# Seven RMS norms of an encoder trunk: the mean of squares and its root over the full tile width instead of one-column sums

## The chip, the core and the metric

The kernel runs on one core of one Trainium2 chip, in one launch. The metric is device time in microseconds (us) from the start of the program to its end; smaller is better. The names of the engines are those of the profile: PE is the matrix engine (TensorE), DVE the vector engine, ACT the scalar engine, POOL is GpSimd, SP issues most of the DMAs. Each engine works through its own queue in order.

## The reference

One encoder layer is applied to two groups of tokens, a prompt of 1024 and a sample of 256, each with 256 memory tokens of its own, at a width of 1024 features, all in fp32.

```python
def rmsnorm(x, w):
    y = x * lax.rsqrt(jnp.mean(x * x, -1, keepdims=True) + EPS)      # EPS = 1e-6
    return y * w

def encoder_layer(x, mem, ...):
    h = rmsnorm(x, norm_mix_w)
    ...                                  # gated DeltaNet and gMLP branches, both of h
    x = x + merged @ w_out
    x = x + memory_cross_attention(rmsnorm(x, norm_xa_w), rmsnorm(mem, norm_mem_w), ...)
    h = rmsnorm(x, norm_ffn_w)
    gu = h @ ffn_w_gate_up
    return x + (silu(gu[..., :D_FF]) * gu[..., D_FF:]) @ ffn_w_down

y = rmsnorm(trunk(x), final_norm_w)      # for prompt and sample
```

The gMLP branch holds a layer norm over 512 features (`layernorm(gelu(v))`), which the change does not touch, but whose instructions stand close to one of the seven norms.

## The kernel before

**Layout.** Features lie on the 128 partitions, in 8 tiles (`k` or `m` from 0 to 7), and tokens along the free axis. The 1280 tokens are cut into three blocks: block 0 and block 1 are 512 prompt tokens each, block 2 is the 256 sample tokens. A norm therefore adds over partitions, and that sum is made on PE.

**Products.** PE multiplies either in fp32 or in the format float32r. Large products are three float32r products: `split` (L124 to L126) has ACT copy a tile to its rounded part `hi` (or `whi`) and DVE or POOL subtract to get the rest `lo` (`wlo`), and PE adds hi·hi, hi·lo and lo·hi in one PSUM bank. Every product goes through `mm`, so nearly all of PE's rows carry line L108.

**A norm before.** `Norm.add` (L240 to L255) squares one of the 8 tiles on ACT into `nsq` (L253; the first directly into the accumulator `nacc`, L250) and adds it to `nacc` on DVE (L254). `Norm.rest` does the remainder, for 512 tokens: four sums of one column each, `nacc` times a column of ones in fp32 (L268; the profile shows two records for each, `bank<-cst,nacc` 128x1); on DVE the mean and EPS (L271) and `rsqrt` (L225 to L230), an integer guess and three Newton steps in ten instructions on 128x4 numbers, into `nst`; four fp32 products with the identity that spread the four columns over all partitions (L276, `bank<-cst,nst` 128x128); then for each of the 8 tiles one DVE product x·w·rstd (L289), and a `sink` that uses the normalised tile (a split into `hi` and `lo` for the products that follow, or a store). With 256 tokens there are two columns instead of four.

**What sets the order.** PE's order is written out by hand: a `main` generator of the large products, and `side` generators, which `pump` resumes when `K.clock`, an estimate of PE's own time advanced by `mm`, has passed the time that they asked for (`yield lag`, in ns). The norms are such side generators; their `lag` and `lag2` place the sums and the spreading products among the large products. The order on DVE, ACT and POOL is made by the scheduler at build, from its own model, so a changed norm can also reorder instructions that are not its own.

**The seven norms that the change touches**, in order of time: x1, the mix norm of block 1 (`norm`, L306 to L312, called at L462, with a lag of 4500); mem, the memory norm (called at L466), whose input `mem` is loaded into the buffer that x1's input leaves (L356, one buffer) and which starts when x1 is done; the FFN norms of blocks 0, 1 and 2 (L1497, in `OutProj.run`), with `inplace`, where the second wait `LAGS2` is 9500 ns for blocks 1 and 2; and the final norms of block 1 and block 0 (L2267), with `LAGF2` 9000. The other norms stay: x0 (L458), the first sample norm (L403 to L424), the three norms of the cross-attention (`rstd_of`, L293) and the final sample norm (L2269 on). The first and the last sample norm already use a seed from ACT (`Abs_reciprocal_sqrt`) and a Newton step over their whole width.

**Neighbours that matter.** While x1 and mem run, PE works on the input products of the gMLP branch, and DVE on its GELU (L487 and L489, `gt` and `ug`) and its layer norm (`ln`, L505 to L518: sums over `vg`, small operations on `sums` 128x4, again `rsqrt` L226 to L230, and at L518 the four wide operations that write `vg`). PE's products `sw`·`vg` (L627) need these. While the FFN norm of block 1 runs, block 2 is still being projected: each of its 8 tiles is added to the residual on DVE (L1462), squared on ACT and added to `nacc` (L254). At the same time POOL splits FFN weights (`wlo<-raw,whi`, 128x1024, L126) and makes four sums of weights (L1847, `raw<-raw`), which the `after` function (L1835 to L1848) issues, and `make_r1` (L1865 to L1869) makes differences of the normalised blocks (L1867, `x<-x,x`) for the FFN's fast product scheme and splits them. In the final norms, half of the eight tiles (`SHARED`) are scaled on ACT and POOL, the others on DVE.

## Time and profile before

| | |
|---|---|
| Time, median of 3 runs (lowest, highest) | 2190.44 us (2190.17, 2190.68) |
| Time of the profiled execution | 2190.45 us |
| Span of the profiled execution | 2188.7 us |
| Granted clock of the core | 0.999 |
| ACT busy | 879.9 us (40%) |
| POOL busy | 569.7 us (26%) |

The span is the time from the first to the last instruction of the profile, 1.75 us less than the execution's own time; the profiled execution is 0.01 us from the median. All times of rows are counted from the start of the span. A row of a group names the line, the engine, the operation, what is written and read (`out<-in`), the shape, the count, then the busy time and the mean duration of one in ns, and idle time ahead of it. A row of the timeline begins with the start and the duration in us; `x4` means that four instructions in a row are put together, the duration reaching from the first start to the last end. Products on PE overlap: what one costs is not its duration but the distance from its start to the start of the next.

### The profile page before, as it was taken

To read this page: it belongs to the slowest core of one execution; us is meant where nothing else is said; L and a number is where in the kernel's file an instruction comes from. 1 tells how busy PE (TensorE), PEld (TensorE's weight loads), DVE (VectorE), ACT (ScalarE), POOL (GpSimd) and SP (SyncE) were. 2 spreads that over 40 slices of the span, in tenths; PEclk is the share of its full clock that TensorE was granted. 3 is DMA by queue.
4 is the path that set the end of the run, shared out by engine and by line. 5 is a ranking of instruction groups with operands and counts; after the bars stand their busy time and mean duration, and the time that the engine had idled before them with its cause. 6 is when DMAs were issued, how large, how long until landed. Compare 5 with 4: busy or idle time off the path is not lost.

```text
span 2188.7 us, 32379 instructions
## 1 busy us (share of the span) xinstructions
PE 2174.0 (99%) x12436; PEld 1905.0 (87%) x12436; DVE 1354.3 (62%) x2614; ACT 879.9 (40%) x1649; POOL 569.7 (26%) x379
## 2 busy tenths in 40 slices
PE   9999999999999999999999999999999999999998
PEld 8988888898888899888988888888888888888888
DVE  7867587686874855677644556644434444378575
ACT  6533262544535553224544533332322323343454
POOL 2010010100000000142412332566666665200031
PEclk9999999999999999999999999999999999999999
DMA  5221412323234546741512521222222222493631
GB/s 194 92 93 58 119 56 91 81 66 93 75 118 126 168 139 202 243 147 39 192 67 97 171 100 63 102 84 87 82 77 78 84 97 92 143 349 120 206 111 58
DMA packets 188309, 255.13 MB, mean 117 GB/s; under 512 B 71978, under 2 KB 102266, under 8 KB 188154
## 3 DMA queue, kind: packets, MB, share of 16 engines
q1 hardware_dynamic: 170618, 228.15, 31.7%
q10 hardware_dynamic: 17536, 24.91, 3.1%
q8 instruction: 97, 1.59, 0.3%
q14 instruction: 58, 0.48, 0.1%
HBM read 179.05 MB, written 73.97 MB: 116 GB/s over the span
## 4 chain that ended last, share of the span: by engine, by line
PE 92%; DVE 5%; ACT 2%; DMA 1%; issue 1%; SPq 0%; POOL 0%; DVEq 0%; ACTq 0%
PE bank L108 91%; PE bank L121 1%; DVE acc L690 1%; DVE U L932 1%; DMA braw<-gq 1%; DMA raw<-in_w_sv 0%; DVE zt L924 0%; ACT U L914 0%; ACT UT L911 0%; DVE nt L289 0%; DVE gb L811 0%; DVE gs L690 0%; ACT junk L513 0%; ACT acc L688 0%; DVE lo L126 0%
## 5 line engine op out<-in xcount | busy, mean ns | idle before, releaser
L108 PE MATMUL bank<-hi,whi 128*128 128x512 f32 (+1 forms) x1976 | 701.2, 355 | 0.2 <-DVE vg L489 0.2
L108 PE MATMUL bank<-lo,whi 128*128 128x512 f32 (+1 forms) x1976 | 686.8, 348 | 0.0
L108 PE MATMUL bank<-hi,wlo 128*128 128x512 f32 (+1 forms) x1976 | 686.8, 348 | 0.0
L108 PEld LDWEIGHTS bank<-hi,wlo 128*128 128x128 f32 x1976 | 373.6, 189 | 48.2
L108 PEld LDWEIGHTS bank<-hi,whi 128*128 128x128 f32 x1976 | 374.4, 189 | 44.4 <-DVE vg L489 1.0
L108 PEld LDWEIGHTS bank<-lo,whi 128*128 128x128 f32 x1976 | 374.5, 190 | 42.8
L125 ACT ACTIVATE whi<-raw 128x1024 fp32r<-128x1024 f32 (+1 forms) x136 | 136.9, 1009 | 248.6 <-PE bank L108 218.9
L126 POOL TENSOR_TENSOR wlo<-raw,whi 128x1024 fp32r<-128x1024 f32 x65 | 158.4, 2439 | 295.5 <-ACT whi L125 295.5
L108 PE MATMUL bank<-bhl,whi 128*128 128x512 f32 x408 | 125.9, 390 | 0.0
L126 DVE TENSOR_TENSOR wlo<-raw,whi 128x1024 fp32r<-128x1024 f32 (+1 forms) x71 | 80.7, 1139 | 70.5 <-ACT whi L125 70.3
L126 POOL TENSOR_TENSOR wlo<-x,whi 128x1024 fp32r<-128x1024 f32 x40 | 96.5, 2412 | 47.5 <-ACT whi L125 47.5
L2107 DVE TENSOR_TENSOR x<-x,bank 128x512 f32<-128x512 f32 x21 | 14.5, 689 | 125.1 <-ACT x L1902 125.1
L690 DVE SCALAR_TENSOR_TENSOR acc<-craw,sm,acc 128x510 f32<-128x510 f32 (+1 forms) x96 | 73.8, 769 | 27.6 <-ACT acc L688 25.9
L108 PEld LDWEIGHTS bank<-bhl,whi 128*128 128x128 f32 x408 | 76.4, 188 | 16.4 <-ACT whi L125 0.4
L1915 DVE SCALAR_TENSOR_TENSOR t<-t,x 128x512 f32<-128x512 f32 x42 | 63.9, 1520 | 28.4 <-ACT t L1914 28.4
L125 ACT ACTIVATE whi<-x 128x1024 fp32r<-128x1024 f32 (+1 forms) x48 | 49.2, 1025 | 77.2 <-PE bank L108 69.3
L108 PE MATMUL bank<-bhl,wlo 128*128 128x512 f32 x204 | 79.6, 390 | 0.5 <-DVE wlo L126 0.5
L108 PE MATMUL bank<-bhl,ahl 128*128 128x512 f32 x312 | 75.0, 395 | 0.0
L1924 DVE SCALAR_TENSOR_TENSOR t<-bank,t 128x512 f32<-128x512 f32 (+1 forms) x44 | 24.5, 558 | 81.4 <-PE bank L108 81.4
L1051 ACT ACTIVATE gs<-bank 128x512 f32<-128x512 f32 (+1 forms) x60 | 31.2, 519 | 103.2 <-PE bank L108 93.8
L1902 ACT ACTIVATE x<-bank 128x512 f32<-128x512 f32 x63 | 37.7, 599 | 82.8 <-PE bank L108 80.1
L108 PEld LDWEIGHTS bank<-bhl,ahl 128*128 128x128 f32 x312 | 58.7, 188 | 13.7
(416 smaller groups left out, 4513.5 us busy)
## 6 DMA issues: line engine op xcount, KB each, us to landing
raw<-in_w_gu SPq DMA_DIRECT2D x44, 512.0 KB, 3.4
braw<-gq SPq DMA_DIRECT2D x14, 1024.0 KB, 6.4
raw<-in_w_g SPq DMA_DIRECT2D x20, 512.0 KB, 3.3
gq<-t SPq DMA_DIRECT2D x33, 256.0 KB, 2.0
gtd<-gs ACTq DMA_DIRECT2D x32, 256.0 KB, 2.4
w<-in_w_dn SPq DMA_DIRECT2D x8, 1024.0 KB, 11.0
raw<-in_w_qkv SPq DMA_DIRECT2D x12, 512.0 KB, 3.5
gq<-r SPq DMA_DIRECT2D x22, 256.0 KB, 2.0
```

Of the source, the lines that this page charges most:

```text
L108: self.nc.tensor.matmul(out, l, r, start=start, stop=stop, skip_group_check=more)
L121: self.nc.tensor.transpose(out, x, ident)
L125: self.last_hi = self.nc.scalar.activation(hi, src, AF.Copy).ins
L126: (eng or self.nc.vector).tensor_tensor(out=lo, in0=src, in1=f32(hi), op=ALU.subtract)
L690: V.scalar_tensor_tensor(out=dst, in0=src, scalar=wj, in1=dst, op0=ALU.mult, op1=ALU.add)
L932: V.scalar_tensor_tensor(out=U[d][:, hs, :], in0=quad(pu), scalar=mine[:, 2 * level + d : 2 * level + d + 1], in1=U[d][:, hs, :], op0=ALU. ...
L1051: S.activation(t, ps, AF.Tanh, scale=0.5)
L1902: S.activation(t, ps, AF.Copy)
L1915: V.scalar_tensor_tensor(out=t, in0=t, scalar=1.0, in1=src, op0=ALU.add, op1=ALU.mult)
L1924: V.scalar_tensor_tensor(out=out, in0=u, scalar=sign, in1=t, op0=ALU.mult, op1=ALU.mult)
L2107: V.tensor_tensor(out=c22, in0=c22, in1=pe, op=ALU.add)
```

## The change

`rest` gets an argument `wide`, set for the seven norms named above. `wide` splits the accumulator at once into two float32r tiles, `nhi` (ACT) and `nlo` (DVE), in the buffers that held squares; waits `lag` + 1500 ns of PE's clock; and makes two products over the whole width with a tile of 1/1024 in all places (`means`, a column `mean_r` read 128 times), whose sum is the mean of squares on every partition. ACT takes the seed of the root of the mean and EPS from it (`Abs_reciprocal_sqrt`), into the accumulator, and DVE makes one Newton step in three wide instructions. The eight products x·w·rstd and the sinks are as before. The four sums of one column, the ten small DVE instructions, the second wait (`LAGS2`, `LAGF2`) and the spreading products go. The `nst` tile of the first part has one buffer instead of two.

```diff
+        def room(self, name, dt=F32):
+            return self.p.tile([P, 512], dt, tag="nsq", name=name, bufs=self.sq)[:, : self.n]
+
+        def wide(self, xk, wcol, sink, pace, shared, lag, ks, inplace, ready):
+
+            n = self.n
+            parts = [self.acc] if self.apart is None else [self.acc, self.apart]
+            hls = []
+            for x in parts:
+                hi, lo = self.room("nhi", F32R), self.room("nlo", F32R)
+                split(hi, lo, x, V)
+                hls += [hi, lo]
+            yield lag + 1500
+            pb = bank()[:, :n]
+            for t in hls:
+                mm(pb, means, t, t is hls[0], t is hls[-1])
+            while ready is not None and not ready():
+                yield 300
+            r = self.acc
+            S.activation(r, pb, AF.Abs_reciprocal_sqrt, bias=eps)
+            V.scalar_tensor_tensor(out=pb, in0=pb, scalar=EPS, in1=r, op0=ALU.add, op1=ALU.mult)
+            V.scalar_tensor_tensor(out=pb, in0=pb, scalar=-0.5, in1=r, op0=ALU.mult, op1=ALU.mult)
+            V.scalar_tensor_tensor(out=pb, in0=pb, scalar=1.5, in1=r, op0=ALU.add, op1=ALU.mult)
...
@@ norm: x1 and mem
-        yield from nm.rest(xk, wcol, sink, pace, lag=lag)
+        yield from nm.rest(xk, wcol, sink, pace, lag=lag, wide=True)
...
+    mean_r = tail.tile([P, 1], F32R, name="mean_r")
+    means = mean_r.to_broadcast([P, P])
     S.activation(h05[:, 12:13], mean, AF.Abs_reciprocal_sqrt)
+    V.tensor_copy(mean_r, mean)
...
@@ the FFN norms of three blocks
-                    norm_b = nms[b].rest(xk, wcol, sinks(b, hs), PACES[b], ks=range(KT) if b != 1 else SECOND_KS, inplace=True, lag2=LAGS2[b])
+                    norm_b = nms[b].rest(xk, wcol, sinks(b, hs), PACES[b], ks=range(KT) if b != 1 else SECOND_KS, inplace=True, wide=True)
...
@@ the final norms of blocks 1 and 0
-            K.side(nm.rest(lambda k: x2[b][:, k, :], S_FIN, sink, PACEF, SHARED[b], LAGF[b], lag2=LAGF2[b]))
+            K.side(nm.rest(lambda k: x2[b][:, k, :], S_FIN, sink, PACEF, SHARED[b], LAGF[b], wide=True))
```

The lines of the changed kernel are up to 42 numbers higher than the old ones (L518 is now L560, L1462 is L1504, L1867 is L1909, the products of L289 are at L328). The change also moves instructions that are not the norms' own. Two places matter below.

**DVE around the gMLP's layer norm of block 0.** `sums` are the small operations of its root (L228 to L230, three Newton steps), `vg` its result, `gt` and `ug` belong to the GELU, and `nacc<-nacc,nsq` are the additions of the mem norm's squares. DVE's queue before:

```order
L228 SCALAR_TENSOR_TENSOR sums<-sums 128x4
L229 TENSOR_TENSOR sums<-sums 128x4
L487 SCALAR_TENSOR_TENSOR gt<-gt,bank 128x512
L230 SCALAR_TENSOR_TENSOR sums<-sums 128x4
L126 TENSOR_TENSOR lo_121<-nt,hi_120 128x512
L228 SCALAR_TENSOR_TENSOR sums<-sums 128x4
L489 SCALAR_TENSOR_TENSOR ug<-gt,bank 128x512
L229 TENSOR_TENSOR sums<-sums 128x4
L230 SCALAR_TENSOR_TENSOR sums<-sums 128x4
L518 TENSOR_SCALAR vg<-vg,sums 128x512 x4
L487 SCALAR_TENSOR_TENSOR gt<-gt,bank 128x512
L254 TENSOR_TENSOR nacc<-nacc,nsq 128x512 x2
```

And of the change, at the same place:

```order
L254 TENSOR_TENSOR nacc<-nacc,nsq 128x512
L229 TENSOR_TENSOR sums<-sums 128x4
L531 SCALAR_TENSOR_TENSOR ug<-gt,bank 128x512
L230 SCALAR_TENSOR_TENSOR sums<-sums 128x4
L254 TENSOR_TENSOR nacc<-nacc,nsq 128x512
L228 SCALAR_TENSOR_TENSOR sums<-sums 128x4
L254 TENSOR_TENSOR nacc<-nacc,nsq 128x512
L229 TENSOR_TENSOR sums<-sums 128x4
L254 TENSOR_TENSOR nacc<-nacc,nsq 128x512
L230 SCALAR_TENSOR_TENSOR sums<-sums 128x4
L254 TENSOR_TENSOR nacc<-nacc,nsq 128x512
L560 TENSOR_SCALAR vg<-vg,sums 128x512 x4
```

Before, the four `vg` stood ahead of all additions of the mem norm; now five of its seven additions stand ahead of them.

**DVE at the end of block 2's projection.** `x_12569` (before) and `x_12549` (after) are block 1, being normalised; `x_12570` and `x_12550` are block 2, whose additions are the 256 wide ones. The queue before, from the last residual addition of block 2 on:

```order
L1462 SCALAR_TENSOR_TENSOR x_12570<-bank,x_12570 128x256
L126 TENSOR_TENSOR lo_12883<-x_12569,hi_12882 128x512 x2
L254 TENSOR_TENSOR nacc<-nacc,nsq 128x256
L289 SCALAR_TENSOR_TENSOR x_12569<-x_12569,sm,bank 128x512
L271 TENSOR_SCALAR bank<-bank 128x2
```

The same stretch of the change, up to the split that the new products of block 2 wait for (`x_12548` is block 0):

```order
L1504 SCALAR_TENSOR_TENSOR x_12550<-bank,x_12550 128x256
L328 SCALAR_TENSOR_TENSOR x_12549<-x_12549,sm,bank 128x512
L126 TENSOR_TENSOR wlo<-x_12549,whi 128x512
L254 TENSOR_TENSOR nacc<-nacc,nsq 128x256
L126 TENSOR_TENSOR wlo<-x_12549,whi 128x512
L328 SCALAR_TENSOR_TENSOR x_12549<-x_12549,sm,bank 128x512
L1504 SCALAR_TENSOR_TENSOR x_12550<-bank,x_12550 128x256
L1909 TENSOR_TENSOR x_12548<-x_12548,x_12549 128x1024
L126 TENSOR_TENSOR wlo<-x_12549,whi 128x512
L254 TENSOR_TENSOR nacc<-nacc,nsq 128x256
L1909 TENSOR_TENSOR x_12548<-x_12548,x_12549 128x1024
L126 TENSOR_TENSOR nlo<-nacc,nhi 128x256
```

Block 1's wide work (its products, their splits and the differences L1909) stood partly behind block 2's last addition; now most of it stands ahead of that addition or of the split `nlo` behind it.

More of the change, by code (lines that the diff above doesn't have):

```diff
@@ L255, in add, with rest @@
             self.k += 1
-        def rest(self, xk, wcol, sink, pace=1300, shared=(), lag=1500, ks=range(KT), inplace=False, ready=None, halves=1, lag2=2800, rooms=()):
+        def rest(self, xk, wcol, sink, pace=1300, shared=(), lag=1500, ks=range(KT), inplace=False, ready=None, halves=1, lag2=2800, rooms=(), wide=False):
             p, n = self.p, self.n
             nb = n // P
+            if wide:
+                yield from self.wide(xk, wcol, sink, pace, shared, lag, ks, inplace, ready)
+                return
             yield lag
@@ L268, in rest @@
                     mm(pc[:, c : c + 1], t[:, c * P : (c + 1) * P], one, t is parts[0], t is parts[-1])
[L269 removed]
+            y = p.tile([P, 4 if p is xp else 16], F32, tag="nst", name="nst", bufs=1 if p is xp else 2)[:, :nb]
             ms, sc = pc[:, 4 : 4 + nb], pc[:, 8 : 8 + nb]
```

13 lines of the change are left out of this document (12 added, 1 removed).

## The prediction, made before the changed kernel was run

> **What bounds the kernel.** I read the page first: busy shares, then the chain that ended last, then PE's own timeline around each norm.
>
> ```profile
> PE 2174.0 (99%) x12436; PEld 1905.0 (87%) x12436; DVE 1354.3 (62%) x2614; ACT 879.9 (40%) x1649; POOL 569.7 (26%) x379
> ...
> PE 92%; DVE 5%; ACT 2%; DMA 1%; issue 1%; SPq 0%; POOL 0%; DVEq 0%; ACTq 0%
> ```
>
> PE is busy 99% of the span and 92% of the chain. So two things count: how long PE takes for the sums, and whether PE now waits for DVE or ACT where it did not. DVE, at 62%, costs nothing unless PE waits for it. PE's timeline at x1:
>
> ```profile
> 55.01 0.28 PE L108 MATMUL bank<-svh,lo 128*128 128x264 f32 x1
> 55.13 0.28 PE L108 MATMUL bank<-svl,hi 128*128 128x264 f32 x1
> 55.25 0.95 PE L108 MATMUL bank<-cst,nacc 128*128 128x1 f32 x8
> 56.06 0.37 PE L108 MATMUL bank<-svh,hi 128*128 128x264 f32 x1
> 56.27 0.28 PE L108 MATMUL bank<-svh,lo 128*128 128x264 f32 x1
> ...
> 59.28 0.28 PE L108 MATMUL bank<-svl,hi 128*128 128x264 f32 x1
> 60.19 1.16 PE L108 MATMUL bank<-cst,nst 128*128 128x128 f32 x8 [0.63 <-DVE nst L230]
> 61.11 0.37 PE L108 MATMUL bank<-svh,hi 128*128 128x264 f32 x1
> ```
>
> A float32r product 264 wide advances PE by 0.12 (55.01 to 55.13). The eight records of the column sums take 56.06 - 55.25 = 0.81, and the product after them 0.21 instead of 0.12: 0.90 in all. The spread takes 61.11 - 60.19 = 0.92 and as much after it, about 1.0, and PE first waits 60.19 - 59.28 - 0.12 = 0.79 for `nst`. x1 thus costs 0.90 + 1.0 + 0.79 = 2.69.
>
> **What PE saves.** An fp32 product of full width (two records), block 1's wait, and the sums of block 2, the smallest norm:
>
> ```profile
> 27.09 1.02 PE L108 MATMUL bank<-sw,cst 128*128 128x512 f32 x2
> ...
> 1330.99 0.28 PE L108 MATMUL bank<-hi,wlo 128*128 128x256 f32 x1
> 1331.35 1.05 PE L108 MATMUL bank<-cst,nacc 128*128 128x1 f32 x8
> ...
> 1351.10 0.50 PE L108 MATMUL bank<-cst,nacc 128*128 128x1 f32 x4
> 1351.46 0.48 PE L108 MATMUL bank<-hi,whi 128*128 128x512 f32 x1
> 1351.78 0.39 PE L108 MATMUL bank<-lo,whi 128*128 128x512 f32 x1
> 1352.01 0.39 PE L108 MATMUL bank<-hi,wlo 128*128 128x512 f32 x1
> ```
>
> A 512 wide float32r product advances PE by 0.23 (1351.78 to 1352.01). No row shows one with the constant as weights; I take that step, 0.454 for the pair of 512, 0.24 for 256. The other end is the fp32 product of the same width, 1.02 at 27.09: it would cost 1.6 more per norm; the format of the pair is float32r, so I stay with the first. Below the step of an ordinary product there is no reason to go.
>
> x1: 2.69 - 0.454 = 2.23. Block 2: sums 0.36 (1351.10 to 1351.46) and 0.09 after, the spread taken as the same, less 0.24: 0.66. Four norms of 512 that do not wait (mem, block 0, both final ones): 0.90 for the sums and, as in block 2, as much for the spread, less 0.454: 1.35 each, 5.4. Block 1 waits 1331.35 - 1330.99 - 0.12 = 0.24, and its eight records take 1.05 instead of 0.95: 1.69. Sum: 2.23 + 0.66 + 5.4 + 1.69 = **10.0 us** off PE.
>
> **First new wait: gMLP, block 0.** DVE's queue now has five of the mem norm's additions ahead of `vg`, and they need mem.
>
> ```profile
> 70.68 0.74 DVE L289 SCALAR_TENSOR_TENSOR nt<-x,sm,bank 128x512 f32<-128x512 f32 x1
> 71.48 1.76 SPq L356 DMA_DIRECT2D mem<-in_memT  x4
> ...
> 74.74 0.68 DVE L487 SCALAR_TENSOR_TENSOR gt<-gt,bank 128x512 f32<-128x512 f32 x1
> 75.34 0.15 DVE L230 SCALAR_TENSOR_TENSOR sums<-sums 128x4 f32<-128x4 f32 x1
> ...
> 76.69 0.63 ACT L250 ACTIVATE nacc<-mem 128x512 f32<-128x512 f32 x1 [0.60 <-DMA mem<-in_memT]
> ...
> 77.12 1.92 DVE L518 TENSOR_SCALAR vg<-vg,sums 128x512 f32<-128x512 f32 x4
> ...
> 77.72 1.86 PE L108 MATMUL bank<-sw,vg 128*128 128x128 f32 x8 [0.41 <-DVE vg L518]
> ```
>
> The load of mem starts when x1's last `nt` frees the buffer (70.68 + 0.74 = 71.42, load at 71.48), and the first square comes 5.21 later, at 76.69. Without the old sums and their wait the last `nt` ends some 1.4 earlier, near 70.0: load at 70.0, square at 75.2, done 75.8, the next square at 76.4. From there DVE walks the queue shown with the change. A wide operation advances DVE by 0.60 (74.74 to 75.34), a small one by 0.15. When the second square is there, the `ug` and the additions still stand in the queue: from 76.45 seven wide operations (two `ug`, five additions) and six small ones until `vg`, 7 x 0.60 + 6 x 0.15 = 5.1, so `vg` starts at 81.55 and PE has the first at about 82.15 (0.60 after the start, as 77.12 to 77.72). PE, 2.23 earlier by x1, would arrive at 77.15 - 2.23 = 74.9 and wait 7.2. Before, it waited 77.72 - 77.15 = 0.57. Against the saving that is **+6.6**. Bounds: 5.4, if DVE catches up two additions while mem comes in, to 7.8, if each addition also waits some tenths for its square.
>
> **Layer norm, block 1 (near 118).** The same walk finds `vg` 0.3 late, behind a POOL weight split; bounds 0 and 2.4, one whole split. I take **+0.3**.
>
> **Second new wait: FFN norm, block 2 (near 1351).** The pair needs `nlo`, which needs the last addition of the squares and, now ahead of it, block 1's normalised tiles and their splits.
>
> ```profile
> 1334.33 2.41 POOL L126 TENSOR_TENSOR wlo<-raw,whi 128x1024 fp32r<-128x1024 f32 x1 [21.64 <-ACT whi L125]
> 1337.21 2.41 POOL L126 TENSOR_TENSOR wlo<-raw,whi 128x1024 fp32r<-128x1024 f32 x1 [0.47 <-ACT whi L125]
> 1339.70 5.59 POOL L1847 TENSOR_TENSOR raw<-raw 128x512 f32<-128x512 f32 x4
> ...
> 1334.59 2.43 DVE L254 TENSOR_TENSOR nacc<-nacc,nsq 128x256 f32<-128x256 f32 x1 [0.23 <-ACT nsq L253]
> 1338.38 1.53 DVE L254 TENSOR_TENSOR nacc<-nacc,nsq 128x256 f32<-128x256 f32 x1 [0.54 <-ACT nsq L253]
> ...
> 1344.23 1.41 DVE L289 SCALAR_TENSOR_TENSOR x<-x,sm,bank 128x512 f32<-128x512 f32 x2
> ...
> 1346.01 1.29 DVE L126 TENSOR_TENSOR lo<-x,hi 128x512 fp32r<-128x512 f32 x2
> ...
> 1348.86 0.42 DVE L1462 SCALAR_TENSOR_TENSOR x<-bank,x 128x256 f32<-128x256 f32 x1
> ...
> 1350.39 0.43 DVE L254 TENSOR_TENSOR nacc<-nacc,nsq 128x256 f32<-128x256 f32 x1
> ```
>
> ```profile
> L1867 DVE TENSOR_TENSOR x<-x,x 128x1024 f32<-128x1024 f32 x2 | 2.4, 1220 | 0.0
> ```
>
> The addition at 1350.39 takes 0.43; the same one at 1334.59 took 2.43 and ended with POOL's split (1334.33 + 2.41 = 1336.74), that at 1338.38 took 1.53 and ended with POOL's next (1339.62). So a DVE operation from two tiles in SBUF that meets a POOL operation ends with it. One that reads PSUM does not: the two at 1344.23 took 0.7 each, beside POOL's sums (1339.70 to 1345.29). In before's times, up to block 1's pair: block 1's `nlo` ends at 1332.7. The next addition meets POOL's first split, moved up to 1333.1, and ends at 1335.8. The Newton step, of three wide operations at 0.66 (the 1344.23 row), with a residual between, ends at 1338.3. The next addition meets POOL's second split and ends at 1339.2; three normalised tiles to 1341.2; their three splits meet POOL's four sums, which hold for 1.4 each, and end at 1345.8. Then 20 DVE operations: four residuals at 0.34, four additions at 0.34, five normalised tiles at 0.66, five splits at 0.60, two L1867 at 1.13: 11.3, so 1357.05, and `nlo` 0.45: **1357.5**. (0.34, 0.60 and 1.13 are my pitches behind the durations 0.42, 0.65 and 1.22 of the rows, less the 0.08 by which starts overlap.) PE gets to the pair, six products later than to the old sums, at 1351.10 - 1.69 + 6 x 0.227 = 1350.8. It waits **+6.7**. Before, the last addition ended at 1350.82 and the sums at 1351.10 did not wait. Bounds: 4.4, if the three splits do not each meet a sum, to 8.0, with one more meeting.
>
> **Final norms.** The applied tiles of block 0 and POOL's four products, no longer 9000 ns behind the sums, meet the splits of the sample's down product.
>
> ```profile
> 2136.44 1.22 DVE L126 TENSOR_TENSOR wlo<-hi,whi 128x512 fp32r<-128x512 f32 x1
> 2138.91 1.72 DVE L126 TENSOR_TENSOR wlo<-hi,whi 128x512 fp32r<-128x512 f32 x1
> ```
>
> Such splits, 0.65 alone, already took 1.22 and 1.72 here, and PE did not wait. I take **+0.5** of 0 to 2. The other three pairs (x1, mem, block 0) and the final one of block 1 find `nlo` done by 0.2 to 1.4 on the same walk: 0.
>
> **Seed and tables.** The seed was measured 256 wide; the next rows show ACT's change of table:
>
> ```profile
> L2275 ACT ACTIVATE seed<-bank,shared 128x256 f32<-128x256 f32 x1 | 0.5, 475 | 0.8 <-PE bank L108 0.8
> ```
>
> ```profile
> 2147.88 1.14 ACT L125 ACTIVATE whi<-w 128x512 fp32r<-128x512 f32 x2
> 2149.04 1.28 ACT L2367 ACT_TABLE_LOAD   x1
> 2150.33 0.30 ACT L2367 ACTIVATE shared<-nacc,shared 128x1 f32<-128x1 f32 x1
> ```
>
> A load takes 1.28, and the work ahead of it and behind it follows without a gap (2147.88 + 1.14 = 2149.02; 2149.04 + 1.28 = 2150.32). There are nine loads instead of three, at most two per norm. Each delays the normalised tiles, which PE needs some microseconds later, and ACT is busy 40%: 0 for PE, with 1.28 as the other end at one place.
>
> The Trainium skill, "ScalarE: Activation LUTs", section "What ACT_TABLE_LOAD costs", counts a drain of about 1380 ns beside the load's 1283 ns. Its load agrees with the 1.28; no drain shows between the rows at 2147.88, 2149.04 and 2150.33, and by it one uncovered change would put the sum 1.4 higher.
>
> **Sum.** -10.0 + 6.6 + 0.3 + 6.7 + 0.5 = +4.1; from 2190.45, the profiled execution (0.01 off the median), **2194.6**. Its own range is 2192 to 2197: the bounds of the waits, not all met at once.
>
> **The rivals.**
>
> *One wait only.* Each rests on a walk of DVE's queue; if one falls (mem's squares come early enough, or block 2's last addition is not held), the time is 2194.6 - 6.7 = 2187.9. For it: 38% of DVE is idle. Against: the queue is in order and both walks pass rows that hold whatever comes behind them.
>
> *No wait: the change is only its saving.* 2190.45 - 10.0 = 2180.5. PE waits almost nowhere in the rows above, so the order would have to have slack of 7 us at two places where before's had 0.57 of wait and 0.28 of slack.
>
> *The change does not do what it says on PE:* the pair with the constant runs at the fp32 pace, 1.6 more for six norms and half for one, 10.4: with both waits 2205. The pair's format speaks against it.
>
> *Slower.* One more POOL split of 2.4 meets a DVE operation ahead of `vg` at 118, or of the pair's split, from the point where POOL's start lies ahead of that operation's: 2194.6 + 2.4 = 2197.0. The row 1334.59 shows that it happens; the starts differ by only tenths of a us.
>
> *Slower, by a table change that stands in the path of PE*, at the seed of block 0 or 1: 2194.6 + 1.3 = 2195.9.
>
> **How the numbers follow.** Both waits 0.52; one wait 0.17; none 0.07; one more POOL meeting 0.17; a table in the path 0.05; fp32 pace 0.02. The bound between change and no change is 0.2%, 4.4 us, about what a measurement of this kernel can tell: 2186.1 and 2194.8. The likeliest case straddles the upper bound, half and half (0.26 each). Slower: 0.26 + 0.17 + 0.05 + 0.02 = 0.50. Faster: no wait 0.07, and 0.03 of one wait, when that one is small. Same: 0.26 + 0.14 = 0.40. The range leaves out the no-wait case, the low end of one wait and the far end of the meetings: 2186 to 2200.
>
> **What would show it.** PE's row of `sw`,`vg` near 77 should carry an idle time of about 7 released by `vg`; the pair of block 2 (`nhi`, `nlo`, 128x256) one of about 6.7 released by `nlo`; each pair should advance PE by 0.23 per product, and the five other pairs should show no idle time over 0.5. No idle at the first two means that the walk of DVE's queue was wrong; pairs at 1.0 per product mean the fp32 pace; a load of tables just ahead of a row on which PE waits means the fifth rival.

## The result, and the profile after

The change takes 2201.78 us (median of six runs, 2201.23 to 2202.06) against 2190.56 for the kernel before (six runs, 2190.17 to 2191.16): a ratio of 1.005 with the 95% interval 1.004 to 1.0061. It is slower by 11.2 us, outside the predicted range. The profiled execution has a span of 2199.9 against 2188.7.

The page after, first its busy shares and then the shares of the chain that ended last:

```profile
PE 2172.3 (99%) x12346; PEld 1899.0 (86%) x12346; DVE 1358.4 (62%) x2566; ACT 895.6 (41%) x1669; POOL 568.1 (26%) x379
...
PE 90%; DVE 6%; ACT 2%; DMA 1%; issue 1%; SPq 0%; DVEq 0%; ACTq 0%
```

PE lost 90 records, and its busy time fell by only 1.7. The chain has 6% of DVE instead of 5%, which is the first sign of PE waiting. PE's own rows at x1 (start, duration, line, result and operands, idle time before it in brackets):

```profile
56.60 0.28 PE L108 MATMUL bank<-svl,hi 128*128 128x264 f32 x1
56.72 0.40 PE L108 MATMUL bank<-nhi,mean_r 128*128 128x512 f32 x1
56.96 0.40 PE L108 MATMUL bank<-nlo,mean_r 128*128 128x512 f32 x1
57.19 0.29 PE L108 MATMUL bank<-svh,hi 128*128 128x264 f32 x1
```

The pair advances PE by 57.19 - 56.72 = 0.47 and PE does not wait for it. Now the layer norm of block 0, PE and then DVE:

```profile
74.87 0.28 PE L108 MATMUL bank<-svl,hi 128*128 128x264 f32 x1
...
81.88 2.17 PE L108 MATMUL bank<-sw,vg 128*128 128x128 f32 x8 [6.73 <-DVE vg L560]
84.06 0.42 PE L108 MATMUL bank<-svh,lo 128*128 128x264 f32 x1
84.28 0.42 PE L108 MATMUL bank<-svl,hi 128*128 128x264 f32 x1
...
123.74 0.94 PE L108 MATMUL bank<-sw,vg 128*128 128x128 f32 x4 [1.07 <-DVE vg L560]
```

```profile
80.67 0.69 DVE L254 TENSOR_TENSOR nacc<-nacc,nsq 128x512 f32<-128x512 f32 x1
...
81.28 1.00 DVE L560 TENSOR_SCALAR vg<-vg,sums 128x512 f32<-128x512 f32 x2
```

The last product ahead of the wait starts at 74.87 and takes a step of 0.12, so PE stands from 74.99 to 81.88: 6.89, where it stood 0.57 before. What holds it is what the prediction named: the last of mem's five additions ends at 80.67 + 0.69 = 81.36, and `vg` follows it in DVE's queue at 81.28 (starts overlap by 0.08). Of the 6.3 that the wait has grown, 2.2 is x1's own saving, which brings PE there earlier, and 4.1 is `vg` coming later.

The last row of PE is block 1's layer norm, with an idle time of 1.07. Counted by starts PE stands 1.2 there and then takes its products at the pace of DVE's `vg`, which makes 1.6. Here one small operation of the root, 0.15 long at block 0, meets a split on POOL and ends with it:

```profile
120.67 2.24 DVE L229 TENSOR_TENSOR sums<-sums 128x4 f32<-128x4 f32 x1
...
120.49 2.39 POOL L126 TENSOR_TENSOR wlo<-raw,whi 128x1024 fp32r<-128x1024 f32 x1 [4.17 <-PE bank L108]
```

The products behind the first wait are slower too: 84.06 to 84.28 is a step of 0.22, where the same products took 0.12 at x1. The table of stretches says why. Its columns are the stretch, its length, busy time and records of PE, PEld, DVE, ACT and POOL, the granted clock of TensorE, and the DMA share and rate:

```profile
79.60:80.09 0.49, 0.00 (x0) 0.00 (x0) 0.46 (x3) 0.32 (x2) 0.00 (x0) 1.00 0.00 0
80.09:86.92 6.83, 5.04 (x22) 5.04 (x23) 6.66 (x13) 1.88 (x4) 0.00 (x0) 0.50 0.00 1
86.92:87.40 0.48, 0.48 (x5) 0.48 (x5) 0.00 (x0) 0.43 (x1) 0.00 (x0) 1.00 0.00 0
...
1360.09:1366.92 6.83, 6.08 (x15) 4.63 (x15) 6.83 (x10) 3.59 (x5) 0.00 (x0) 0.50 0.30 101
```

At each of the two long waits TensorE is granted half its clock for 6.83 us, beginning before the wait ends. The pair of block 2, PE and DVE:

```profile
1354.72 0.39 PE L108 MATMUL bank<-hi,wlo 128*128 128x512 f32 x1
...
1360.41 0.58 PE L108 MATMUL bank<-nhi,mean_r 128*128 128x256 f32 x1 [5.30 <-ACT nhi L125]
1361.42 0.58 PE L108 MATMUL bank<-nlo,mean_r 128*128 128x256 f32 x1 [0.43 <-DVE nlo L126]
1361.80 0.63 PE L108 MATMUL bank<-hi,whi 128*128 128x512 f32 x1
1362.22 0.63 PE L108 MATMUL bank<-lo,whi 128*128 128x512 f32 x1
```

```profile
1345.17 4.58 DVE L126 TENSOR_TENSOR lo<-x,hi 128x512 fp32r<-128x512 f32 x3
...
1359.48 0.41 DVE L254 TENSOR_TENSOR nacc<-nacc,nsq 128x256 f32<-128x256 f32 x1
1359.81 1.21 DVE L1909 TENSOR_TENSOR x<-x,x 128x1024 f32<-128x1024 f32 x1
1360.95 0.41 DVE L126 TENSOR_TENSOR nlo<-nacc,nhi 128x256 fp32r<-128x256 f32 x1
```

PE waits 1360.41 - (1354.72 + 0.23) = 5.46 for `nhi` and 1361.42 - 1360.41 - 0.12 = 0.89 for `nlo`, 6.35 in all; both need block 2's last addition. Three splits of block 1 take 4.58 beside POOL's sums (1345.17), and block 2's last addition comes only at 1359.48. The 512 wide step behind it is 1362.22 - 1361.80 = 0.42, not 0.23.

The rest of the time was followed through the lag: the start of the same copy or product in the trace after less that in the trace before. It gives each term of the sum by itself:

| term | predicted | measured from the lag |
|---|---|---|
| sums gone, seven pairs instead | -10.0 | -9.8 |
| wait at block 0's layer norm | +6.6 | +6.3 |
| half clock behind it | none | +1.7 |
| wait at block 1's layer norm (123.74) | +0.3 | +1.6 |
| 1080 to 1240 | none | -0.6 |
| wait at block 2's FFN norm | +6.7 | +6.35 |
| half clock behind it | none | +2.6 |
| 1400 to 2080, lag grows evenly from 10.9 to 12.8 | none | +1.9 |
| final norms, small waits of 0.10 to 0.17 at 2126 to 2136 | +0.5 | +1.1 |
| sum | +4.1 | +11.2 |

### The profile page after: what moved, and what is told of

Same layout as the page of the kernel before. It is cut to its first block, busy times and chain, and to the rows that moved or that the text cites. A ratio compares the mean times of both kernels' runs of the same rounds, so it can differ in the third digit from the quotient of the medians.

```text
span 2199.9 us, 32170 instructions
## 1 busy us (share of the span) xinstructions
PE 2172.3 (99%) x12346; PEld 1899.0 (86%) x12346; DVE 1358.4 (62%) x2566; ACT 895.6 (41%) x1669; POOL 568.1 (26%) x379
## 4 chain that ended last, share of the span: by engine, by line
PE 90%; DVE 6%; ACT 2%; DMA 1%; issue 1%; SPq 0%; DVEq 0%; ACTq 0%
PE bank L108 89%; PE bank L121 1%; DVE acc L732 1%; DVE U L974 1%; DMA braw<-gq 1%; DVE nacc L254 0%; DVE lo L126 0%; DVE zt L966 0%; ACT U L956 0%; DVE x L328 0%; ACT UT L953 0%; DMA xs<-in_xT 0%; DVE wlo L126 0%; DVE gb L853 0%; DVE gs L732 0%
```

## The experiments

Two experiments have a single run each; every other one was timed against the kernel before on its own chip. There before's single runs spread over 2189.6 to 2193.9, so a difference below some two microseconds is read from the lag in the traces, not from the medians. Four questions were asked: what the two waits hang on, what the steady loss after 1400 is, when the clock halves, and whether some of the norms are worth making wide.

### The two waits

**The additions of mem's squares behind `vg`.** The square and its addition are issued only once block 0's last `vg` is.

```diff
-            nm.add(xk(k))
+            with tc.issue_after(behind()):
+                nm.add(xk(k))
...
-            V.tensor_scalar(out=vg[:, c, :], ...)
+            last = V.tensor_scalar(out=vg[:, c, :], ...)
+        done_ln[cs.start // 4] = last.ins
```

> The change with mem's squares and additions put behind the four vg operations of block 0's layer norm in the queues, nothing else. Theory A (PE's wait of 6.9 at 74.9 is DVE's queue, and the half clock that follows it, 0.50 from 81 to 87, is a consequence of the wait): the wait falls to 0.6 to 1.0, no slice near 80 has a clock under 1.0, and the time falls by 6.0 + 2.0 = 8.0, to 2193.8. Theory B (the low clock has another cause): only the wait goes, 2195.8. Theory C (the work ahead of vg is only pushed to the next wait): PE waits for the mem pair or at 122 instead, 2198 to 2202.

Measured: 2199.00, ratio 1.0037 [1.0024, 1.005]. The wait did not go; it fell from 6.89 to 4.15, and the lag at 130 from 6.14 to 3.34. ACT, DVE and PE:

```profile
71.01 0.72 ACT L561 ACTIVATE junk<-vg,sums 128x512 f32<-128x512 f32 x1 [0.15 <-DVE sums L557]
...
73.98 0.17 DVE L562 TENSOR_SCALAR sums<-sums 128x4 f32<-128x4 f32 x1 [2.26 <-ACT junk L561]
...
78.83 2.17 PE L108 MATMUL bank<-sw,vg 128*128 128x128 f32 x8 [3.99 <-DVE vg L566]
```

DVE idles 2.26 ahead of the layer norm's root (2.27 in the trace after), for ACT's squares of `vg`, which begin at 71.01, and at 69.41 in before. They begin late because the sums that they need stand behind x1's own wide tiles in DVE's queue: x1's Newton step, three operations of 512 after a load of ACT's table, ends at 61.8 in the changed kernel, and its eight products and their splits follow. So the place of mem's additions is 2.74 of the wait, and what is left, 4.15 against the 0.57 of before, goes back to x1's wide path: some 2.1 of it is x1's saving, by which PE comes earlier, and the rest is `vg` coming later. At a wait of 4.15 the clock is halved too, from 77.57 to 84.40.

**Block 1's FFN pair later**, so that its normalised tiles, their splits and the L1909 stand behind block 2's additions, as before. Only the planner's delay of block 1 goes from 1500 to 9500 ns.

```diff
-    norm_b = nms[b].rest(..., inplace=True, wide=True)
+    norm_b = nms[b].rest(..., inplace=True, wide=True, lag=(1500, 9500, 1500)[b])
```

> The change with the two products of FFN norm block 1 asked for 8000 ns later on PE, where its spreading products stood before, nothing else. Theory A (block 1's tiles, splits and differences stand in DVE's queue ahead of block 2's nlo, and the half clock from 1360 to 1367 follows from PE's wait of 5.5 and 0.9): PE waits under 1.5 at block 2's pair, the clock stays at 1.0, and the time falls by about 5 + 3.2 = 8.2, to 2193.6. Theory B (clock of another cause): 2196.8. Theory C (POOL's splits hold block 2's additions whatever stands in the queue): the wait stays above 4, 2200.

Measured: 2194.99, ratio 1.0018 [1.0009, 1.0027]. The pair's waits are 1.13 and 0.34, and the clock stays whole:

```profile
1356.84 0.39 PE L108 MATMUL bank<-nhi,mean_r 128*128 128x256 f32 x1 [0.97 <-ACT nhi L125]
```

```profile
1354.00:1362.00 8.00, 6.96 (x31) 5.33 (x30) 7.99 (x17) 5.61 (x10) 0.00 (x0) 1.00 0.39 132
```

The lag at 1400 is 4.87 instead of 10.93; allowing for a lag that was already 0.76 higher ahead of the place, the edit takes 6.8 out. Of this 6.35 - 1.47 = 4.9 is wait and 2.6 the clock behind it; near 1391 PE now loses some 0.6 that it did not lose in the trace after.

### The steady loss after 1400

From 1400 to 2080 no product waits longer than before and the clock is 1.00, yet the lag grows by 1.9. The changed kernel's new constant and its one `nst` fewer move later tiles in SBUF, many by 32 or 96 bytes.

**Every moved tile at a multiple of 64 bytes**, in the same order of instructions:

```diff
-            y = p.tile([P, 4 if p is xp else 16], F32, tag="nst", name="nst", bufs=1 if p is xp else 2)[:, :nb]
+            y = rstd[:, :nb] if p is xp else p.tile([P, 16], F32, tag="nst", name="nst", bufs=2)[:, :nb]
-    mean_r = tail.tile([P, 1], F32R, name="mean_r")
+    mean_r = tail.tile([P, 16], F32R, name="mean_r")[:, 0:1]
```

> The change with mean_r 64 instead of 32 bytes wide and the first norm's nst put into free columns of another tile, so that every SBUF tile that the change moved lies again a multiple of 64 bytes from its place before. The order on every engine is that of the change. Theory A (the steady loss between 1400 and 2080, where the changed kernel falls 10.9 to 12.8 us behind the old one with no wait of PE, comes of tiles moved by 32 or 96 bytes): 1.8 us less than the change, 2200.0; the lag stays at 10.9 to 11.0 over that stretch. Theory B (the loss comes of traffic or of the clock): the time of the change, 2201.8, and the lag grows as there.

Measured: 2201.89, ratio 1.005 [1.0033, 1.0067]. A miss: the lag still grows, from 10.4 to 12.8. The granule of 64 bytes does not decide it.

**The three edits so far together:**

> All three edits together. If the three losses are independent: 2201.8 - 1.8 - 8.0 - 8.2 = 2183.8, faster than before by 6.6 us. If removing one wait lets another take its place: 2187 to 2192.

Measured: 2192.42, ratio 1.0008 [0.9998, 1.0017]. That is far from 2183.8, the sum of three independent losses: the two waits' edits add up, but the first takes out only 2.8 of 8.0 and the third nothing. The lag at the end is 1.1, and the loss after 1400 is 2.1, as large as ever.

**The same order of instructions as in the three, but every old tile where it lies in the kernel before**; the constant takes the room that `nst` has left, in each pool apart:

```diff
-    mean_r = tail.tile([P, 16], F32R, name="mean_r")[:, 0:1]
-    means = mean_r.to_broadcast([P, P])
+    def means_in(p):
+        if id(p) not in held:
+            m = p.tile([P, 8 if p is xp else 32], F32R, tag="mean_r", name="mean_r", bufs=1)
+            V.tensor_copy(m[:, :1], mean)
+            held[id(p)] = (p, m[:, :1].to_broadcast([P, P]))
+        return held[id(p)][1]
```

> The three edits of e4, but the column of 1/1024 now lies, one for each pool, in the room that the old nst tiles left, so that every other SBUF tile has exactly the address that it had in the kernel before; the order on every engine is that of e4. e1 let tiles lie 64 bytes off and the steady loss between 1400 and 2080 stayed (2.3 us there). Theory A2 (the loss comes of which addresses PE reads together, in steps finer or coarser than 64 bytes): the loss of 2.0 us that e4 has in that stretch goes to 0 to 0.2, and the time is 2.0 us under e4's, 1 us under before. Theory B (it is not the addresses): the stretch loses 2.0 as in e4, and so the time is e4's.

Measured: 2191.09 against 2191.17, ratio 1.0001 [0.9992, 1.0011]. The loss is gone: from 1400 to 1900 the lag stays at 0.67. Near 1910 it jumps by 0.5, where PE waits for a split of weights (`wlo`). With the old places that jump differs from run to run, from -0.5 to +1.6, and the rest of the stretch stays flat.

**And the reverse: the kernel before, with nothing but wider `nst` tiles**, which lay x0, x1, x2, `t4` and others 64 bytes lower; the order on every engine is that of before:

```diff
-            y = p.tile([P, 4 if p is xp else 16], F32, tag="nst", name="nst", bufs=2)[:, :nb]
+            y = p.tile([P, 4 if p is xp else 24], F32, tag="nst", name="nst", bufs=2)[:, :nb]
```

> The kernel before with nothing changed but the room of nst, 96 bytes for 64, so that the tiles x0, x1, x2 and t4 and the buffers beside them lie 64 bytes lower; the order on every engine is that of before. Theory A2 (which addresses PE reads together sets its pace in the FFN): the lag against before is 0 until 1400 and grows (or shrinks) steadily by 1 to 3 us from 1400 to 2080, at a clock of 1.0 and without a wait. Theory B (the loss in that stretch came of something that the change itself does): no lag, the time of before within 0.3.

Measured: 2192.22 against 2191.12, ratio 1.0004 [0.9995, 1.0013]. The traces are clearer than the times. Here stand two of ACT's copies out of PSUM, the 7th and the last of 63 in a part of the FFN where PE never waits, in before, after, the kernel with old places, and this one:

```profile
1429.55 0.60 ACT L1902 ACTIVATE x<-bank 128x512 f32<-128x512 f32 x1 [1.34 <-PE bank L108]
...
1890.77 0.60 ACT L1902 ACTIVATE x<-bank 128x512 f32<-128x512 f32 x1 [2.27 <-PE bank L108]
```

```profile
1440.54 0.60 ACT L1944 ACTIVATE x<-bank 128x512 f32<-128x512 f32 x1 [1.34 <-PE bank L108]
...
1903.08 0.60 ACT L1944 ACTIVATE x<-bank 128x512 f32<-128x512 f32 x1 [2.27 <-PE bank L108]
```

```profile
1430.22 0.60 ACT L1958 ACTIVATE x<-bank 128x512 f32<-128x512 f32 x1 [1.34 <-PE bank L108]
...
1891.44 0.60 ACT L1958 ACTIVATE x<-bank 128x512 f32<-128x512 f32 x1 [2.27 <-PE bank L108]
```

```profile
1429.82 0.60 ACT L1902 ACTIVATE x<-bank 128x512 f32<-128x512 f32 x1 [1.34 <-PE bank L108]
...
1892.48 0.60 ACT L1902 ACTIVATE x<-bank 128x512 f32<-128x512 f32 x1 [2.27 <-PE bank L108]
```

The same work takes 461.22 in before, 462.54 after, 461.22 with the new instructions at the old places, and 462.66 with the old instructions at shifted places. In all nine traces with the old places the stretch takes 461.22, and in all six with shifted ones 462.54 to 462.90. So the places of the tiles alone make the loss. In the trace after, the mean step of the 512 wide products `t4h`·`whi` has grown from 229.8 ns to 235.4, of `t4h`·`wlo` from 227.0 to 231.7, and of the others by about 1 at most.

### When the clock halves

**Stops of four lengths put into the kernel before.** Ahead of four of the FFN's parts PE fills a bank, ACT copies that bank over itself 2, 4, 6 or 10 times, and PE fills it again, so PE stands meanwhile. Nothing of the computation changes.

```diff
+            if f in PAUSES:
+                pk = bank()
+                hold(1, pk)
+                for _ in range(PAUSES[f]):
+                    S.activation(pk, pk, AF.Copy)
+                hold(1, pk)
             yield from ff_up(f)
...
+PAUSES = {5: 2, 9: 4, 13: 6, 17: 10}
```

> The kernel before, with four stops put on PE in the FFN's up stage, far apart: an fp32 product of zeros into a bank, then 2, 4, 6 and 10 copies of that bank onto itself on ACT, one behind the other, then a product into it again. PE should stand still for about 1.5, 2.7, 3.9 and 6.3 us. Theory A (a stop of PE itself makes the clock low, beyond a length between 1.3 and 4): the clock stays at 1.0 after the first, and falls to 0.50 after the third and fourth, for 3 to 7 us, which costs 1.7 to 3.5 us each beyond the stop. Theory B (the low clock at 80 and 1360 had another cause): the clock stays at 1.0 after all four.

Measured: 2222.12, a single run. The stops are 2.1, 3.33, 4.56 and 7.0 long. The first two with the stretches behind them:

```profile
1480.13 1.13 PE L389 MATMUL bank<-shared 128*128 128x512 f32 x2 [1.74 <-ACT bank L2133]
...
1584.57 1.99 PE L389 MATMUL bank<-shared 128*128 128x512 f32 x2 [2.96 <-ACT bank L2133]
```

```profile
1482.00:1486.00 4.00, 4.00 (x25) 3.51 (x24) 2.80 (x2) 0.60 (x1) 2.28 (x2) 1.00 0.09 33
...
1584.00:1588.00 4.00, 3.43 (x6) 2.09 (x7) 3.92 (x3) 0.52 (x1) 3.37 (x3) 0.59 0.04 9
...
1692.00:1696.00 4.00, 4.00 (x8) 2.48 (x9) 2.02 (x2) 0.00 (x0) 1.51 (x1) 0.50 0.17 66
```

The stop of 2.1 leaves the clock whole, and the other three do not. So a wait alone, with no change of work, halves the clock. The Trainium skill, "TensorE: Matmul & The Clock Gate", section "What's actually happening", has a clock of half rate after an idle window of about 3.4 us and a window that runs freely. The 0.50 of the rows agrees, and so do the stops of 4.56 and 7.0; the one of 3.33 is shorter than that window and still halves the clock.

**Four stops of 2.1 and four of 3.33 at other places.**

```diff
-PAUSES = {5: 2, 9: 4, 13: 6, 17: 10}
+PAUSES = {3: 2, 6: 2, 9: 2, 11: 2, 13: 4, 15: 4, 17: 4, 19: 4}
```

> The kernel before with eight stops of PE in the FFN's up stage, four behind 2 copies (2.1 us each in e8) and four behind 4 (3.4). e8's stop of 2.1 left the clock at 1.0, but e12's wait of 1.86 was followed by a clock of 0.50. Theory A (a free-running window decides, so stops of one length differ): of the four short ones some are followed by half clock and some not, and the stretch at half clock differs by up to 3 us between stops of one length. Theory B (the length of the stop decides alone): all four short ones leave the clock at 1.0, all four long ones cost the same within 0.3.

Measured: 2230.68, a single run. All four short stops leave the clock at 1.00. Of the long ones three halve it for a while and one, near 1807, does not; one of the three, and that one:

```profile
1751.00:1758.00 7.00, 6.70 (x27) 5.01 (x28) 3.66 (x3) 0.85 (x2) 3.18 (x2) 0.76 0.10 37
...
1807.00:1814.00 7.00, 6.48 (x32) 5.27 (x33) 3.90 (x3) 1.06 (x2) 3.33 (x3) 1.00 0.10 39
```

So near 3.3 us the moment decides beside the length. The next two show the same with a wait that the kernel makes itself.

**x1's norm as before, mem's alone wide** (on top of the kernel with the old places):

```diff
-        yield from nm.rest(xk, wcol, sink, pace, lag=lag, wide=True)
+        yield from nm.rest(xk, wcol, sink, pace, lag=lag, wide=behind is not None)
```

> e5 with x1's norm made the old way (column sums, spread, no table change); mem, FFN and final norms stay wide. Theory A (e2's wait of 4.1 that was left is x1's: its nine table and Newton steps put its tiles ahead of the layer norm's sums in DVE's queue, 69.7 instead of 68.0): PE's wait for vg is back at 0.6, the one at 119 to 122 (1.2) goes too, no low clock near 80; against e5 the time falls by 3.6 + 1.2 + about 2 for the clock, less the 2.1 that x1 saved: 4 to 5. Theory B (mem alone holds vg): the wait stays near 4, the time rises by 2.

Measured: 2191.85 against 2191.17, ratio 1.0004 [0.9995, 1.0014]. The wait at block 0's layer norm is back at 0.56, which agrees with x1's part in it, and the clock stays whole there. But a wait of 3.36 stands at 117, for `gm`: mem's normalised tiles come later, and DVE's work for the decays behind them meets both of POOL's splits (two small operations take 2.40 and 2.32 there). The first row below is block 0's, the second the new one:

```profile
77.60 0.49 PE L108 MATMUL bank<-sw,vg 128*128 128x128 f32 x2 [0.40 <-DVE vg L573]
...
117.42 0.63 PE L108 MATMUL bank<-cst,gm 128*40 128x128 f32 x4 [3.21 <-DVE gm L613]
```

```profile
117.00:121.00 4.00, 3.58 (x21) 2.67 (x22) 3.79 (x18) 1.44 (x3) 0.00 (x0) 1.00 0.33 121
```

**The same, with block 0's final pair 7500 ns later**, to see whether the small waits near 2130 are its doing:

```diff
-            K.side(nm.rest(..., SHARED[b], LAGF[b], wide=True))
+            K.side(nm.rest(..., SHARED[b], LAGF[b] + (7500 if b == 0 else 0), wide=True))
```

> e6 with the final norm's pair of block 0 asked for 7500 ns later on PE, where its spread stood before. Theory A (the small waits of 0.1 to 0.17 from 2125 to 2136, 1.2 in all, are the sample's splits meeting the normalised tiles and POOL's products): they go, 1.2 less than e6. Theory B (the later norm ends late and holds the end): 1 to 3 more than e6.

Measured: 2192.24, ratio 1.0006 [0.9997, 1.0015]. The small waits stayed, and two new ones of 0.69 and 0.38 came near 2148, so the delay was no cure. The trace shows one thing more. Ahead of the final norms every engine has the order of the experiment before, with the same wait, 3.36, at the same place, and this time the clock halved:

```profile
117.00:121.00 4.00, 3.62 (x15) 3.11 (x16) 3.79 (x18) 1.25 (x3) 0.00 (x0) 0.50 0.30 116
```

15 records instead of 21 in four microseconds, and a lag at 130 of 4.14 instead of 2.30. The same wait in the same program thus costs 1.84 more or nothing more, as it falls; the last section says how it falls. The lag of this run at the end, 4.42, also holds a jump of 1.55 at the split near 1910.

### Which norms are worth it

**x1 as before; mem wide without a delay; block 2's pair 3500 instead of 1500 ns behind; all at the old places.**

```diff
-  yield from norm(xp, ..., behind=lambda: done_ln.get(0))
+  yield from norm(xp, ..., wide=True, lag=-1500)
...
-  lag=(1500, 9500, 1500)[b])
+  lag=(1500, 9500, 3500)[b])
```

> Tile addresses as before; x1 the old way; mem wide with its pair 3000 ns earlier on PE (before the late tiles of mem met POOL's splits and the decays' chain behind them, PE's wait of 3.4 at 114 in e6); block 1's FFN pair 8000 ns later as in e3, block 2's 2000 ns later; final norms wide. Theory A (every wait that the change brought comes of where the pair stands and what its tiles push in DVE's queue): no wait over 0.6 beyond those of before up to 1390, no low clock; the sum is -1.3 (mem) -1.35 -1.7 -0.66 (FFN) -2.7 +1.2 (final): 6.5 under before. Theory B (a wide norm's longer chain of table, seed and three Newton steps always finds something behind it): a wait of 2 to 4 appears at 100 to 120 again, 0 to 3 under before.

Measured: 2193.01 against 2191.12, ratio 1.0008 [0.9999, 1.0017]. At block 0's layer norm nothing waits longer than before, though mem is wide and its additions are no longer held back: with x1 as before the planner puts them behind `vg` of its own accord. So the whole first wait has its root in x1's wide path. But mem's earlier pair waits 1.0 for its splits near 90, and at block 1's layer norm PE loses 0.8, so that mem's wide norm gains nothing. At 1385 the lag is -3.2, the best so far. Then PE waits 2.88 and 1.35 for block 2's own tiles, which now come too late for the next products, and half the clock follows; the lag rises to +2.78. PE's rows at both places:

```profile
77.64 1.86 PE L108 MATMUL bank<-sw,vg 128*128 128x128 f32 x8 [0.41 <-DVE vg L567]
...
1390.26 0.50 PE L108 MATMUL bank<-whi 128*128 128x512 f32 x1 [2.72 <-ACT x L1951]
```

**The same with mem as before:**

```diff
-  yield from norm(xp, ..., wide=True, lag=-1500)
+  yield from norm(xp, ...)
```

> As e9, but mem too is made the old way, so that the first 130 us are those of the kernel before. Theory A: until 130 the lag is 0 within 0.2; the FFN norms give 3.7, the final ones 1.5: 5.2 under before. Theory B (waits appear in the FFN part again): 1 to 3 under before.

Measured: 2192.64, ratio 1.0006 [0.9997, 1.0015], with the same waits at 1387 to 1390 and a lag of 3.2 at the end, 1.2 of it from the split near 1910. Delaying block 2's pair was an error of both.

**x1, mem and block 2 as before; blocks 0 and 1 and both final norms wide, block 1 late.**

```diff
-  wide=True, lag=(1500, 9500, 1500)[b])
+  wide=b < 2, lag=(1500, 9500, 1500)[b], lag2=LAGS2[b])
```

> Wide only where nothing is behind: FFN norms of blocks 0 and 1 (block 1's pair 8000 ns later, as in e3) and the two final norms; x1, mem and block 2 the old way; all other tiles at the addresses of the kernel before. Theory A: no wait beyond those of before and no low clock anywhere; -1.35 -1.7 for the two FFN norms and -2.7 +1.2 for the final ones: 4.5 under before, 0.998 of it. Theory B (delayed or not, a wide norm in the FFN part brings a wait, as block 2's pair did at 1387 in e9 and e10): 0 to 2 under before.

Measured: 2190.12 against 2191.58, ratio 0.9992 [0.9983, 1.0001]. That is 1.5 of the 4.5 us that were hoped for. The old sums of block 2 wait 1.86, and though that is short, the clock behind it is not whole:

```profile
1349.67 0.61 PE L108 MATMUL bank<-cst,nacc 128*128 128x1 f32 x4 [1.70 <-DVE nacc L254]
```

```profile
1351.00:1355.00 4.00, 4.00 (x12) 3.12 (x11) 3.97 (x9) 1.87 (x3) 0.00 (x0) 0.57 0.43 152
```

**Only block 0 of the FFN norm and the two final norms wide.**

```diff
-  wide=b < 2, lag=(1500, 9500, 1500)[b], lag2=LAGS2[b])
+  wide=b == 0, lag2=LAGS2[b])
```

> Wide for block 0's FFN norm and the two final norms alone; x1, mem, blocks 1 and 2 the old way and at the old places; tile addresses as before. Theory A (the saving of PE itself is real, and only what the wide norms of x1, mem, block 1 and block 2 push in DVE's queue eats it): no new wait at 1347 or 1387, no low clock; -1.35 at 1300 and -1.5 at the end: 2.9 under before. Theory B (the wide norm of block 0 moves the load to a later wait too, as block 1's did in e12): 0 to 1 under before.

Measured: **2188.29 against 2191.21, ratio 0.9986 [0.9977, 0.9995]**, faster than the kernel before by an interval that leaves out 1, and the only one of the experiments of which that can be said. From 80 us on there is no new wait and no halved clock, and to the end the lag falls by 2.8; in this execution the clock was halved once earlier, from 28.16 to 31.57 (see the last section). The stretch between the two copies is 461.22 again. Its page:

```profile
PE 2171.8 (99%) x12394; PEld 1902.0 (87%) x12394; DVE 1357.1 (62%) x2595; ACT 885.1 (40%) x1657; POOL 568.3 (26%) x379
```

**And without block 0's final norm:**

```diff
-  LAGF[b], wide=True))
+  LAGF[b], lag2=LAGF2[b], wide=b == 1))
```

> As e13, with the final norm of block 0 the old way too. Theory A (its 1.35 is eaten by the meetings with POOL from 2113 to 2125, 1.2): -1.35 -1.35, so 2.7 under before, the same as e13 within 0.3. Theory B (those small waits belong to the other final norm): 1.5 under before, and the waits of 0.16 stay.

Measured: 2189.62 against 2191.21, ratio 0.9992 [0.9983, 1.0001]. The lag falls by 1.35 at block 0 and only 0.3 net at the final norm: the small waits of 0.16 are still there, so they come with block 1's final norm, not with block 0's.

## Why the prediction was wrong

Its likeliest case, both waits, is what happened. Taken alone, its terms as measured give -9.8 + 6.3 + 1.6 + 6.35 + 1.1 = +5.55, or 2196.0, inside the range. The steps that failed are two that the sum did not have.

- **Behind a wait it let PE go on at its old pace.** "It waits +6.7" and "against the saving that is +6.6" end with the wait. The halved clock then took 1.7 and 2.6 more, 4.3 of the 7.1 that the sum is short of. That a wait halves the clock is shown by the stops in the kernel before, and that it costs by two executions of the same wait, 1.84 apart.
- **It counted instructions and not where their operands lie.** The constant and the missing `nst` move later tiles, and between 1400 and 2080 that costs 1.9, less the 0.6 gained from 1080 to 1240: 1.3 net. Both go when the tiles are put back, and in the FFN stretch the shift alone brings the loss, 1.44 in 461.

Two terms were too small within their bounds. Block 1's layer norm was put at 0.3 of 0 to 2.4 and measured 1.6, by the POOL split that the prediction named there; the final norms at 0.5 of 0 to 2 and measured 1.1, in small waits that come with block 1's norm, not in block 0's meeting with the sample's splits as the prediction had it. Block 0's `vg` and block 2's pair were 0.65 too large together.

- **The saving was right:** 10.0 against 9.8. The pair of 512 took 0.45 to 0.48 against 0.454, so the fp32 pace is ruled out.
- **The first walk of DVE's queue was right in its count:** seven wide and six small operations, `vg` at 81.55 predicted and 81.28 measured, PE's arrival 74.9 and 74.99. That its start was right is luck. It began at 76.45 because mem's second square would be done then; in the trace after that square ends at 76.76, before DVE comes to its addition at 76.95, and DVE has been busy with hardly a gap since 74.27, when the layer norm's root began (72.36 in before). So the cause lay one step further back. The prediction took mem's additions as what moved; holding them back saved 2.74 of the wait, while x1 as before took away all of it, with mem's additions held back or not.
- **The second walk was right** in its mechanism, that block 1's wide work ahead of block 2's last addition is what PE waits for, since moving that work alone took the wait from 6.35 to 1.47. The three splits did meet POOL's sums (4.58 for three). Its rule that a DVE operation which meets one of POOL ends with it is right to some tenths: in its own row at 1334.59 the addition ends at 1337.02, POOL's split at 1336.74.
- **Tables:** no load stands just ahead of a row on which PE waits, so the fifth rival did not come. Loads do stand further back on x1's and mem's chains (at 57.44 and 59.70, 96.81 and 99.20); what they cost PE by that was not measured by itself.

Of the rivals one came in part: the POOL split did meet an operation of DVE ahead of `vg` near 118, but PE lost 1.6 by it and not 2.4, and without the halved clock the time would have stayed within the range. No wait fell away, and the pair runs at its format's pace.

Not settled: which places of tiles make products slow (a multiple of 64 bytes is not enough to be well off), why one-column products seem to count as idle for the clock, and what exactly makes the small waits at block 1's final norm.

## What to carry to other kernels

A shorter sum on PE pays only where its operands are ready early: the three norms whose pair found its splits done made the kernel 0.14% faster, while the other four cost more in waits than all seven saved. Put a price on a PE wait of some microseconds that is its length and about two more for the halved clock behind it (1.7, 1.84 and 2.6 here), and look at what is queued in front of the releaser on DVE, not at how idle DVE is on average. When a change adds or removes a tile, keep the others at their places before judging it, or the places' own effect is taken for the change's.

## What the runs showed of the hardware that was not expected

- **The clock.** At every wait of 4.15 and more the granted clock fell to 0.50; of seven waits and stops of 3.3 to 3.4, five had this and two had not; five stops of 2.1 had not. Yet the wait of 1.86 at block 2's old sums was followed by a mean of 0.57 over 1351 to 1355, beginning after PE had gone back to work. The Trainium skill, "TensorE: Matmul & The Clock Gate", section "Why this matters for your kernels", warns of gaps longer than about 3 us; the waits of 4.15 and more and five of the seven agree, the one of 1.86 does not, and the measurement decides: a wait well below that can cost the clock as well.
- **What decides it.** In each trace with several falls of the clock they lie whole multiples of 3.413 us apart, and the clock stays low for 3.41 or 6.83 us (once 10.24), or to the end of the program. By an estimate from the PE rows of all traces, it falls where PE was idle for about 2.0 us or more of the 3.41 ahead of such a point, if the time of one-column products counts as idle: 1.96 or more ahead of each fall between 10 and 2170 us, at most 1.98 ahead of the points without one. That they count as idle is argued from these traces and was not tested by itself. The wait of 3.36 at 117 was cut by a point at 116.02 the first time (counted back from that trace's only fall, at 2184.50), with 1.96 ahead of it, and at 116.58 the second, with 2.55. The wait of 1.86 has 1.49 in its stretch, and four one-column sums with it make 1.96. The clock also fell with hardly any wait, in three executions near 28 us; here are the rows of the fastest kernel, PE's sixteen one-column records and then the stretches before and after the fall:

```profile
24.68 1.94 PE L108 MATMUL bank<-cst,squares 128*128 128x1 f32 x16
```

```profile
24.75:28.16 3.41, 3.21 (x22) 2.36 (x22) 2.14 (x11) 3.10 (x8) 3.41 (x2) 1.00 0.33 109
28.16:31.57 3.41, 3.41 (x17) 3.41 (x18) 3.23 (x20) 1.08 (x3) 0.05 (x1) 0.50 0.56 201
```

- **The places of tiles in SBUF.** 64 bytes of shift, with every instruction the same, made 461.22 us of pure products 462.66. The 1.44 us are half of what the better kernel gains in all.
